# Low halves of weights by accumulating DMA, seven Strassen chunks in layer 0, and a new split of the modulation columns

## The chip, the cores and the metric

One Trainium2 chip; the program runs on one core. The metric is the device time of that core in microseconds (us), from runs of the whole program. TensorE is PE in the profile, VectorE DVE, ScalarE ACT, GpSimd POOL; SP is the queue from which almost all DMAs are issued.

## The reference

Two layers of an encoder trunk on 512 tokens of width 1024, all in float32. Each layer is a mixer (attention in two branches) and an MLP; both norms are modulated by `mod`, 6 x 1024 values for each layer that depend on `c` and `ada_w` alone.

```python
for l in range(DEPTH):
    mod = (cond @ ada_w[l] + ada_b[l])[:, None, :]
    shift_m, scale_m, gate_m, shift_f, scale_f, gate_f = jnp.split(mod, 6, axis=-1)
    h = rms_norm(x, norm_mix_g[l]) * (1.0 + scale_m) + shift_m
    proj = h @ w_in[l]
    ...
    x = x + gate_m * y
    h = rms_norm(x, norm_mlp_g[l]) * (1.0 + scale_f) + shift_f
    x = x + gate_f * (jnp.square(jax.nn.relu(h @ w_mlp_up[l])) @ w_mlp_down[l])
```

`w_mlp_up` is 1024 x 4096 and `w_mlp_down` 4096 x 1024.

## The kernel before

**Split operands.** PE multiplies in a format shorter than float32 (`R32`, fp32r). So each operand is held in two parts: a high part, rounded by a copy on ACT (`wh <- raw`), and the rest, subtracted on DVE (`wl <- raw, wh`). `split_w` does this for a weight block of 128 x 1024 (512 KB): SP loads `raw`, ACT writes `wh`, DVE writes `wl`. `mm3` makes a product from three matmuls: high by high, high by low, low by high. The pool of `raw` tiles has 4 buffers (`rawp`), that of `wh`, `wl` pairs 5 (`wp`).

**Columns.** `ada(l, j)` makes column j of the 48 columns of `mod`: SP loads 512 KB of `ada_w` into a `raw` tile, and DVE multiplies it by `cbc` and sums (`CUSTOM_DVE_ANT_0`, then a short read of the accumulator). Columns 0 to 15 of layer 1 must be there at the end of layer 0's MLP, the others at the end of layer 1's attention.

**Attention.** Each layer goes through some 60 slots in an order that is written out by hand for every engine (`order(True)`): parts of a projection, parts of attention of earlier slots, and what `mods` and `mods1` put at the slot's end. `mods1` gives layer 1 its columns 24 to 47, one at every second slot from 6 to 52.

**MLP.** 32 up tiles (`up_part`: 8 x 3 = 24 matmuls of 512 columns for each) are worked in 8 chunks of 4. What follows in a chunk is of one of two kinds, by `PLAIN[l] <= fc < 7`, with `PLAIN = (3, 0)`:

- A plain chunk: ReLU, square and split of the 4 tiles, then 8 sums over the 4 tiles in 96 matmuls; each result is multiplied by the gate on DVE and added to x on POOL. In layer 0 each of the chunks 0 to 2 ends with 8 columns of layer 1 (`INFF // PLAIN[l]`, 24 in all). The last chunk is plain in both layers.
- A Strassen chunk: `columnside` loads the four down blocks r11, r12, r21, r22 (r21 and r22 into the pool of `raw` tiles) and makes three differences of them on DVE. `rowside` makes and splits the row side. `down7` makes seven products of 12 matmuls each in the order r11, r21, t2, t1, t3, r22 and r21 - t2, splits the right side of each (`wsplit`: ACT, then DVE), and takes the results from PSUM on DVE into the sums `y` (`take`). Before `down7`, two up tiles of the next chunk are made.

Layer 0 had 4 such chunks (3 to 6), layer 1 had 7 (0 to 6). In the MLP no order is written out: a scheduler sets it when the program is built. Each engine then works its instructions in that fixed order, and waits on semaphores for the others; SP waits in the same way for a free buffer before it issues a load.

**PSUM.** `acc()` counts its calls and takes turns over 2 banks of one pool and 3 of another; `ubank()` gives up tiles others.

Of the kernel before, what the change touches and what calls it, by code (L numbers as in the profile page):

```python
# [10 lines left out]
F32 = mybir.dt.float32  # L11
R32 = mybir.dt.float32r
BF = mybir.dt.bfloat16
I32 = mybir.dt.int32
AF = mybir.ActivationFunctionType
OP = mybir.AluOpType
AX = mybir.AxisListType

DEPTH = 2
# [22 lines left out]
def trunk(ctx, tc, x, c, pos, cols, rows, ada_w, w_qkv, w_gate, w_ba, w_bb, w_out, w_up, w_down, out):  # L42
# [8 lines left out]
    rawp = pool("raw", 4)  # L51
    wp = pool("w", 5)
# [196 lines left out]
    def split_w(src, n=1024, scale=None, eng=None, spare=False):  # L249
        raw = rawp.tile([128, 1024], F32, name="raw", tag="raw")  # L250
        E_.dma_start(raw[:, :n], src)
        if spare:
            hi, lo = (big([128, 1024], R32, n_) for n_ in ("wh", "wl"))
        else:
            hi, lo = (wp.tile([128, 1024], R32, name=n_, tag=n_) for n_ in ("wh", "wl"))
        if scale is None:
            S_.activation(hi[:, :n], raw[:, :n], AF.Copy)
            (eng or V_).tensor_sub(lo[:, :n], raw[:, :n], hi[:, :n].bitcast(F32))
        else:
            S_.activation(hi[:, :n], raw[:, :n], AF.Copy, scale=scale)  # L260
            V_.scalar_tensor_tensor(lo[:, :n], raw[:, :n], scale, hi[:, :n].bitcast(F32),
                                           op0=OP.mult, op1=OP.subtract)
        return hi, lo

    def mm3(o, sh, sl, mh, ml, start, stop, **more):
# [331 lines left out]
    TURN = 18  # L597
    FIRST = 0
    AHEAD = 4
    PLAIN = (3, 0)  # L600
    INFF = 24

    def halves(hT):

# [111 lines left out]
    for l in range(DEPTH):  # L716
# [97 lines left out]
            loads.setdefault((k - 1, 1), []).append(slots[k]["load"])  # L814
        mods = {k: 16 + i for i, k in enumerate(range(54, 62))}
        MODS = len(mods)
        mods1 = {6 + 2 * i: INFF + i for i in range(48 - INFF)}
        post1_at, post2_at, turn_at = {}, {}, {}
        for k in range(nq):
            at = k + 1 if k >= done else STRIDE * k + done + FIRST  # L820
# [131 lines left out]

        def up_part(j, lo, hi):
            if j not in up:
                up[j] = [split_w(w_up[l, j])]
            if lo == 0:
                up[j].append(acc() if j < max(EARLY, FCH * PLAIN[l]) else ubank())
            (wh, wl), ps = up[j]
            hs = slice(lo, hi)
            for kt in range(KT):  # L960
                kc = slice(128 * kt, 128 * kt + 128)
                mm3(ps[:, hs], wh[:, kc], wl[:, kc], hF[kt][0][:, hs], hF[kt][1][:, hs], kt == 0, kt == KT - 1)
            return ps
# [15 lines left out]
        def product(banks, u, w, start):  # L979

            wh, wl = w
            for i, ps in enumerate(banks):
                for k in range(2):
                    tk = slice(256 * k + 128 * i, 256 * k + 128 * i + 128)
                    cw = slice(512 * k, 512 * k + 512)
                    mm3(ps, u[:, 0, tk], u[:, 1, tk], wh[:, cw], wl[:, cw], start and k == 0, k == 1,
                        skip_group_check=not start)
# [61 lines left out]
            V_.tensor_sub(r12, r22, r12)  # L1049
            return r11, r21, t2, t1, r12, r22  # L1050

        def down7(fc, u, b):

            def wsplit(raw):
                hi, lo = (wp.tile([128, 1024], R32, name=n_, tag=n_) for n_ in ("wh", "wl"))
                S_.activation(hi, raw, AF.Copy)
                V_.tensor_sub(lo, raw, hi.bitcast(F32))
                return hi, lo  # L1060

            r11, r21, t2, t1, t3, r22 = b

            def take(y, ps):
                if y not in ys:
                    ys[y] = [halfp.tile([128, 512], F32, name="y7", tag="half") for _ in range(2)]
                    for yt, b in zip(ys[y], ps):
                        S_.activation(yt, b, AF.Copy)
                else:
                    for yt, b in zip(ys[y], ps):  # L1070
                        V_.tensor_add(yt, yt, b)

            bank = lambda pool_, tag: [pool_.tile([128, 512], F32, name="acc", tag=tag) for _ in range(2)]
            xb, yb = bank(ssp, "s"), bank(tpp, "tp")
            if not zb:
                zb.extend(bank(accp, "acc"))
            product(xb, u[1], wsplit(r11), True)
            take((0, 0), xb)
            w21 = wsplit(r21)
            V_.tensor_sub(r21, r21, t2)  # L1080
            product(zb, u[2], w21, fc == PLAIN[l])
            product(xb, u[6], wsplit(t2), False)
            take((0, 1), xb)
            product(yb, u[5], wsplit(t1), True)
            take((1, 1), yb)
            product(xb, u[7], wsplit(t3), False)
            take((1, 1), xb)
            product(yb, u[3], wsplit(r22), False)
            take((0, 1), yb)
            product(xb, u[4], wsplit(r21), False)  # L1090
            take((1, 0), xb)

        for fc in range(FC):
            last = fc == FC - 1
            if seven(fc):
                w7 = columnside(fc)
            ups(fc, (2, 3) if fc and seven(fc - 1) else range(FCH))
            if fc == 0:
                gf = grow(l, 1)
            if seven(fc):  # L1100
                u7 = rowside(fc)
                ups(fc + 1, (0, 1))
                down7(fc, u7, w7)
                continue
            if last:
                for b, y in zip(zb, ys[0, 0]):
                    V_.tensor_add(y, y, b)
                for (i, cc), y2 in sorted(ys.items()):
                    for k, y in enumerate(y2):
                        xs = slice(512 * cc, 512 * cc + 512)  # L1110
                        V_.tensor_mul(y, y, gf[:, xs])
                        G_.tensor_add(x1[2 * i + k][:, xs], x1[2 * i + k][:, xs], y)
            if last and l + 1 < DEPTH:
                nxt = prepare(l + 1)
                for i in range(2):
                    nxt[1][0]["load"](i, True)
            for cc in range(2):
                w = [split_w(w_down[l, fc, cc, i]) for i in range(2)]
                if last and l + 1 < DEPTH and cc == 0:
                    nxt[1][0]["load"](2)  # L1120
                ahead = last and cc == 1 and l + 1 < DEPTH
                if ahead:
                    pairs = halves(nxt[0])
                    aT = affine(l + 1, 0)
                    norms = []
                    order(True)
                    nxt[1][0]["load"](3)
                for t in range(NT):
                    tk = slice(128 * t, 128 * t + 128)
                    d = sp.tile([128, 512], F32, name="d", tag="f512", bufs=6)  # L1130
                    final = last and l == DEPTH - 1 and cc == 1 and t == NT - 1
                    for lo, hi in ((0, 256), (256, 512)) if final else ((0, 512),):
                        ps = acc()[:, lo:hi]
                        for f in range(FCH):
                            wh, wl = w[f // 2]
                            cw = slice(512 * (f % 2) + lo, 512 * (f % 2) + hi)
                            mm3(ps, uT[f][:, 0, tk], uT[f][:, 1, tk], wh[:, cw], wl[:, cw], f == 0, f == FCH - 1)
                        xs = slice(512 * cc + lo, 512 * cc + hi)
                        V_.tensor_mul(d[:, lo:hi], ps, gf[:, xs])
                        (V_ if last else G_).tensor_add(x1[t][:, xs], x1[t][:, xs], d[:, lo:hi])  # L1140
                        if last and l == DEPTH - 1:
                            E_.dma_start(out[t, :, xs], x1[t][:, xs])
                    if last and l + 1 < DEPTH and cc == 0:
                        ms[t] = msp.tile([128, 2], F32, name="ms2", tag="ms")
                        square(x1[t], ms[t], 0)
                    if ahead:
                        norms.append(norm(l + 1, 0, t, x1[t], ms[t], aT, pairs))
                        if t > 1:
                            norms[t - 2][2]([0])
                        norms[t][0]()  # L1150
                        E_.dma_start(x2d[t], x1[t])
                        if t > 0:
                            norms[t - 1][1]()
                        if t > 1:
                            norms[t - 2][2]([1])
                if ahead:
                    norms[3][1]()
                    early = {1 + i: norms[2 + i][2] for i in range(2)}
            if l + 1 < DEPTH and not last:
                n = INFF // PLAIN[l]  # L1160
                for i in range(n * fc, n * fc + n):
                    ada(l + 1, i)


_ORDER = ["x", "c", "pos", "cols", "rows", "ada_w", "w_qkv", "w_gate", "w_ba", "w_bb", "w_out", "w_up",
# [64 lines left out]
```

## Time and profile before

| | |
|---|---|
| three runs | 1893.67, 1893.89, 1896.83 us; median 1893.89 |
| the profiled execution | 1896.49 us, of which the span of its instructions 1894.7 |
| busy, share of the span | PE 1857.2 us (98%), DVE 1382.4 (73%), ACT 934.6 (49%), POOL 407.0 (21%) |
| mean granted TensorE clock | 0.995 |
| HBM read | 205.09 MB |
| chain that ended last | PE 70%, DVE 15%, ACT 7%, DMA 3% |

By time: the first norm and projection up to about 95 us, layer 0's attention to 425, its gates and output projection to 600, its MLP to about 950, layer 1's attention to 1370, its gates and output projection to 1560, its MLP to the end.

PE's matmuls overlap in the profile (one of 512 columns shows as 389 ns, and one follows the other every 0.22 to 0.23 us), so a stretch of PE is judged by the number of matmuls in it. A group's mean is the mean time of one instruction; the idle time before it is the engine's wait, with what ended it.

### The profile page before, as it was taken

How to read it: one execution, taken by the hardware profiler on the slowest of the kernel's cores; microseconds unless marked ns; L12 is line 12 of the kernel's file. 1: busy time of each engine (PE TensorE's matmuls, PEld its weight loads, DVE VectorE, ACT ScalarE, POOL GpSimd, SP SyncE). 2: the span in 40 equal slices, each digit the busy share in tenths (PEclk: the TensorE clock that was granted, in tenths of full speed). 3: DMA queues.
4: the chain of work that ended last, by engine and by line, in shares of the span. 5: the costliest groups of instructions: out<-in, count | busy, mean ns of one | idle time of the engine just before them, and what ended most of it. 6: DMA issues, size and time to landing. Idle time of an engine off the chain costs nothing.

```text
span 1894.7 us, 27435 instructions
## 1 busy us (share of the span) xinstructions
PE 1857.2 (98%) x10012; PEld 1636.7 (86%) x10012; DVE 1382.4 (73%) x2721; ACT 934.6 (49%) x2009; POOL 407.0 (21%) x463
## 2 busy tenths in 40 slices
PE   7999999999999999999998999999999999999999
PEld 5999999998878888888898999988888888888887
DVE  8776678886586767688977676888743457788887
ACT  5555566666334432544454545666662345444441
POOL 4332324332121223000243231332310100000002
PEclk9999999999999999999999989999999999999999
DMA  7321111225583656322233231232232333332322
GB/s 297 138 68 58 52 54 48 70 65 156 181 288 122 200 189 205 96 89 89 78 123 121 86 112 57 84 101 81 66 112 89 100 126 107 104 108 89 111 68 88
DMA packets 63640, 212.10 MB, mean 112 GB/s; under 512 B 7185, under 2 KB 7569, under 8 KB 63506
## 3 DMA queue, kind: packets, MB, share of 16 engines
q1 hardware_dynamic: 63218, 210.27, 34.6%
q8 instruction: 79, 1.29, 0.3%
q14 instruction: 55, 0.45, 0.1%
q10 hardware_dynamic: 288, 0.09, 0.0%
HBM read 205.09 MB, written 5.24 MB: 111 GB/s over the span
## 4 chain that ended last, share of the span: by engine, by line
PE 70%; DVE 15%; ACT 7%; DMA 3%; issue 2%; POOL 2%; SPq 0%; ACTq 0%; DVEq 0%; POOLq 0%
PE acc L81 61%; PE tp L81 3%; DVE wl L81 3%; PE s L81 3%; DVE raw L81 2%; ACT p L81 2%; ACT wh L81 2%; PE pvb L81 2%; PE pv L81 2%; DVE T L81 1%; DVE kl L81 1%; DVE y L81 1%; DVE ms L81 1%; DVE nm L81 1%; POOL rs L81 1%
## 5 line engine op out<-in xcount | busy, mean ns | idle before, releaser
L81 PE MATMUL acc<-wh,hT 128*128 128x384 f32 x1792 | 518.5, 347 | 9.0 <-ACT hT L81 5.2
L81 DVE TENSOR_TENSOR wl<-raw,wh 128x1024 fp32r<-128x1024 f32 (+1 forms) x325 | 381.6, 1182 | 182.9 <-ACT wh L81 179.7
L81 PE MATMUL acc<-hT,wh 128*128 128x512 f32 (+1 forms) x1632 | 481.6, 378 | 0.0
L81 ACT ACTIVATE wh<-raw 128x1024 fp32r<-128x1024 f32 (+1 forms) x325 | 315.7, 986 | 331.3 <-PE acc L81 217.7
L81 PEld LDWEIGHTS acc<-hT,wh 128*128 128x128 f32 x1632 | 298.5, 188 | 54.6
L81 PEld LDWEIGHTS acc<-wh,hT 128*128 128x128 f32 x1792 | 330.6, 189 | 16.0 <-ACT hT L81 6.6
L81 PE MATMUL acc<-hT,wl 128*128 128x512 f32 (+1 forms) x816 | 306.0, 378 | 1.3 <-DVE wl L81 1.3
L81 PE MATMUL acc<-wl,hT 128*128 128x384 f32 x896 | 303.6, 339 | 3.7 <-DVE wl L81 3.7
L81 PE MATMUL acc<-wh,uT 128*128 128x512 f32 (+1 forms) x944 | 296.1, 388 | 0.2 <-DVE d L81 0.2
L81 POOL TENSOR_TENSOR rs<-ms,half_neg 128x4 f32<-128x4 f32 (+1 forms) x128 | 123.1, 962 | 493.5 <-DVE ms L81 492.3
L81 PEld LDWEIGHTS acc<-wh,uT 128*128 128x128 f32 x944 | 176.8, 188 | 37.3 <-DVE d L81 0.6
L81 PE MATMUL acc<-wl,uT 128*128 128x512 f32 (+1 forms) x472 | 182.5, 387 | 0.0
L81 PEld LDWEIGHTS acc<-hT,wl 128*128 128x128 f32 x816 | 153.5, 188 | 30.8 <-DVE wl L81 2.6
L81 PEld LDWEIGHTS acc<-wl,hT 128*128 128x128 f32 x896 | 169.7, 189 | 9.2 <-DVE wl L81 6.6
L81 DVE CUSTOM_DVE_ANT_0 raw<-raw,cbc,colt 128x1024 f32<-128x1024 f32 x94 | 123.5, 1322 | 18.2 <-DMA raw<-in_ada_w 17.9
L81 ACT ACTIVATE p<-s,nm 128x512 f32<-128x512 f32 x128 | 86.9, 684 | 86.7 <-DVE nm L81 86.7
L81 POOL TENSOR_TENSOR xt<-xt,y 128x512 f32<-128x512 f32 x16 | 26.2, 1651 | 461.3 <-DVE y L81 461.3
L81 PEld LDWEIGHTS acc<-wl,uT 128*128 128x128 f32 x472 | 88.6, 188 | 17.9
L81 DVE TENSOR_REDUCE nm<-s 128x1 f32<-128x512 f32 x128 | 82.1, 682 | 16.4 <-PE s L81 16.3
L81 ACT ACTIVATE sq<-acc 128x256 f32<-128x256 f32 x112 | 43.2, 385 | 87.2 <-DVE kl L81 67.7
L81 PE MATMUL s<-k,q 128*128 128x512 f32 (+1 forms) x224 | 84.8, 386 | 1.3 <-DVE n L81 1.3
L81 ACT ACTIVATE wT<-tp 128x512 f32<-128x512 f32 (+1 forms) x128 | 65.8, 541 | 39.7 <-PE tp L81 39.5
(157 smaller groups left out, 2884.3 us busy)
## 6 DMA issues: line engine op xcount, KB each, us to landing
raw<-in_ada_w SPq DMA_DIRECT2D x96, 512.0 KB, 4.1
raw<-in_w_qkv SPq DMA_DIRECT2D x112, 384.0 KB, 3.1
raw<-in_w_up SPq DMA_DIRECT2D x64, 512.0 KB, 3.8
raw<-in_w_down SPq DMA_DIRECT2D x64, 512.0 KB, 3.5
raw<-in_w_gate SPq DMA_DIRECT2D x32, 512.0 KB, 3.6
raw<-in_w_ba SPq DMA_DIRECT2D x16, 512.0 KB, 3.6
raw<-in_w_out SPq DMA_DIRECT2D x16, 512.0 KB, 3.6
xt<-in_x SPq DMA_DIRECT2D x8, 512.0 KB, 6.2
```

What stands on the lines that cost most here:

```text
L81: ins = f(*a, **k)
```

## The change

Five things change.

1. `split_add` takes the place of `split_w` for the up tiles that `up_part` loads (29 of 32 in each layer; the first three are loaded elsewhere, as before). ACT writes `wh`, then a second ACT instruction writes -`wh` into `wl`, and a DMA issued by POOL adds the weight block from HBM onto `wl`. DVE has no part in it.
2. In `down7` the blocks r11 and r22, which are multiplied as they are loaded, are split in the same way.
3. `PLAIN = (0, 0)`: layer 0's chunks 0 to 2 become Strassen chunks, so that it has 7.
4. `INFF = 35`: layer 0's MLP makes 35 of layer 1's columns, five in each Strassen chunk, one after each of the first five takes as the code is written (`idle`).
5. Layer 1's attention makes the other 13, one at every fourth slot from 6 to 54.

```diff
+    def split_add(src):
+
+        raw = rawp.tile([128, 1024], F32, name="raw", tag="raw")
+        E_.dma_start(raw, src)
+        hi, lo = (wp.tile([128, 1024], R32, name=n_, tag=n_) for n_ in ("wh", "wl"))
+        S_.activation(hi, raw, AF.Copy)
+        S_.activation(lo, hi.bitcast(F32), AF.Copy, scale=-1.0)
+        G_.dma_start(lo, src, accum_op=OP.add)
+        return hi, lo
...
-    PLAIN = (3, 0)
-    INFF = 24
+    PLAIN = (0, 0)
+    INFF = 35
...
-        mods1 = {6 + 2 * i: INFF + i for i in range(48 - INFF)}
+        mods1 = {6 + 4 * i: INFF + i for i in range(48 - INFF)}
...
-                up[j] = [split_w(w_up[l, j])]
+                up[j] = [split_add(w_up[l, j])]
...
-        def down7(fc, u, b):
+        def down7(fc, u, b, rest):
...
-            def wsplit(raw):
+            def wsplit(raw, src=None):
                 hi, lo = (wp.tile([128, 1024], R32, name=n_, tag=n_) for n_ in ("wh", "wl"))
                 S_.activation(hi, raw, AF.Copy)
-                V_.tensor_sub(lo, raw, hi.bitcast(F32))
+                if src is None:
+                    V_.tensor_sub(lo, raw, hi.bitcast(F32))
+                else:
+                    S_.activation(lo, hi.bitcast(F32), AF.Copy, scale=-1.0)
+                    G_.dma_start(lo, src, accum_op=OP.add)
                 return hi, lo
+
+            def idle():
+                if rest:
+                    rest.pop(0)()
...
-            product(xb, u[1], wsplit(r11), True)
+            product(xb, u[1], wsplit(r11, w_down[l, fc, 0, 0]), True)
             take((0, 0), xb)
+            idle()
...
-            product(yb, u[3], wsplit(r22), False)
+            product(yb, u[3], wsplit(r22, w_down[l, fc, 1, 1]), False)
             take((0, 1), yb)
+            idle()
...
-                down7(fc, u7, w7)
+                down7(fc, u7, w7, [lambda i=i: ada(l + 1, i) for i in range(5 * fc, 5 * fc + 5)] if l + 1 < DEPTH else [])
...
-            if l + 1 < DEPTH and not last:
-                n = INFF // PLAIN[l]
-                for i in range(n * fc, n * fc + n):
-                    ada(l + 1, i)
```

In the built program this makes 86 DMAs on POOL (58 up tiles and 28 down blocks) and 86 more instructions on ACT for the negations; PE has 36 matmuls less. The scheduler then puts the MLP in an order of its own. Three places of that order, with the numbers of the tiles; `wh_N` and `wl_N+1` are the halves of one block.

ACT before, in chunk 4 of layer 0, from the split of t3 (raw_8333) over r22 (raw_8337) and r21 - t2 (raw_8336) to the next up tiles and r11 (raw_8641):

```order
L81 ACTIVATE wh_8587<-raw_8333 128x1024
L81 ACTIVATE r_8509<-acc_8484 128x512
L81 ACTIVATE wh_8605<-raw_8337 128x1024
L81 ACTIVATE wh_8623<-raw_8336 128x1024
L81 ACTIVATE wh_8656<-raw_8654 128x1024
L81 ACTIVATE wh_8691<-raw_8689 128x1024
L81 ACTIVATE wh_8754<-raw_8752 128x1024
L81 ACTIVATE wh_8789<-raw_8787 128x1024
L81 ACTIVATE wh_8825<-raw_8641 128x1024
```

ACT now, at that place of chunk 2 of layer 0 (a plain chunk before), from the split of r22 (raw_7703) over r21 - t2 (raw_7702) to three of the four up tiles:

```order
L81 ACTIVATE wh_7988<-raw_7703 128x1024
L81 ACTIVATE r_7879<-acc_7854 128x512
L81 ACTIVATE wl_7989<-wh_7988 128x1024
L81 ACTIVATE wh_8010<-raw_7702 128x1024
L81 ACTIVATE wh_8043<-raw_8041 128x1024
L81 ACTIVATE wl_8044<-wh_8043 128x1024
L81 ACTIVATE wh_8079<-raw_8077 128x1024
L81 ACTIVATE wl_8080<-wh_8079 128x1024
L81 ACTIVATE wh_8143<-raw_8141 128x1024
L81 ACTIVATE wl_8144<-wh_8143 128x1024
```

Behind each split of an up tile, and of r22, stands its negation; the next split waits for both.

DVE before, in chunk 4 of layer 0 again, from the split of r21 - t2 (wl_8624) on: takes, and between them the splits of the next chunk's up tiles (wl_8657, wl_8692, wl_8755, wl_8790):

```order
L81 TENSOR_TENSOR wl_8624<-raw_8336,wh_8623 128x1024
L81 TENSOR_TENSOR y7_8272<-y7_8272,acc_8514 128x512
L81 TENSOR_TENSOR y7_8252<-y7_8252,acc_8512 128x512
L81 TENSOR_TENSOR y7_8253<-y7_8253,acc_8513 128x512
L81 TENSOR_TENSOR y7_8273<-y7_8273,acc_8515 128x512
L81 TENSOR_TENSOR wl_8657<-raw_8654,wh_8656 128x1024
L81 TENSOR_TENSOR y7_8252<-y7_8252,acc_8514 128x512
L81 TENSOR_TENSOR wl_8692<-raw_8689,wh_8691 128x1024
```

DVE now, between chunks 1 and 2 of layer 0, from the end of the takes: three columns (ISA, two instructions for each), the split of r21 (wl_7909), the square of an up tile, a low half of the row side, the difference r21 - t2, and the next two columns:

```order
L81 TENSOR_TENSOR y7_7365<-y7_7365,acc_7553 128x512
L81 ISA raw_7943,modT1_105<-raw_7943,cbc_96,colt_101 128x1024
L81 ISA modT1_105 128x1
L81 ISA raw_7964,modT1_105<-raw_7964,cbc_96,colt_101 128x1024
L81 ISA modT1_105 128x1
L81 TENSOR_TENSOR wl_7909<-raw_7702,wh_7908 128x1024
L81 SCALAR_TENSOR_TENSOR q7_7745<-acc_7718,r_7743 128x512
L81 TENSOR_TENSOR uT_7786<-q7_7515,uT_7786 128x512
L81 TENSOR_TENSOR raw_7702<-raw_7702,raw_7701 128x1024
L81 ISA raw_7985,modT1_105<-raw_7985,cbc_96,colt_101 128x1024
L81 ISA modT1_105 128x1
L81 ISA raw_8007,modT1_105<-raw_8007,cbc_96,colt_101 128x1024
```

Where splits of up tiles stood there are now columns; the first of the five stands just ahead of these rows. The code has the columns between the products, the built order has them together, behind the takes.

PE before, in chunk 4 of layer 0, inside the product of r22 (wh_8605): two matmuls of the next chunk's first up tile (wh_8656), then the product of t3 (wh_8587):

```order
L81 MATMUL acc_8514<-wl_8606,uT_8437 128x512
L81 MATMUL acc_8514<-wh_8605,uT_8437 128x512
L81 MATMUL acc_8660<-hT_6432,wh_8656 128x512
L81 MATMUL acc_8660<-hT_6433,wh_8656 128x512
L81 MATMUL acc_8512<-wh_8587,uT_8433 128x512
L81 MATMUL acc_8512<-wl_8588,uT_8433 128x512
```

The tile's third matmul, the first to read its low half wl_8657, followed after 18 others. PE now, in chunk 2, behind the product of t1 (wl_7947): two matmuls of the next chunk's first up tile, and the product of t3 (wh_7967):

```order
L81 MATMUL acc_7885<-wl_7947,uT_7797 128x512
L81 MATMUL acc_7885<-wh_7946,uT_7797 128x512
L81 MATMUL acc_8048<-hT_6432,wh_8043 128x512
L81 MATMUL acc_8048<-hT_6433,wh_8043 128x512
L81 MATMUL acc_7882<-wh_7967,uT_7801 128x512
L81 MATMUL acc_7882<-wl_7968,uT_7801 128x512
```

The two read `wh_8043` alone. The up tile's other 22 matmuls, the first of which reads `wl_8044`, now follow after 38 others: the products of t3, r22 and r21 - t2 (12 each) and two matmuls of the second up tile.

More of the change, by code (lines that the diff above doesn't have):

```diff
@@ L1083, in down7 @@
             take((0, 1), xb)
+            idle()
             product(yb, u[5], wsplit(t1), True)
             take((1, 1), yb)
+            idle()
             product(xb, u[7], wsplit(t3), False)
             take((1, 1), xb)
-            product(yb, u[3], wsplit(r22), False)
+            idle()
+            product(yb, u[3], wsplit(r22, w_down[l, fc, 1, 1]), False)
             take((0, 1), yb)
+            idle()
             product(xb, u[4], wsplit(r21), False)
```

## The prediction

> **What bounds the kernel now.** I read the slices of the page first, then busy time by stretches, one Strassen chunk or one group of attention slots to a stretch. Columns: the stretch and its length, busy us (xinstructions) of PE, PEld, DVE, ACT and POOL, granted clock, DMA share, GB/s.
>
> ```profile
> 663.00:757.00 94.00, 94.00 (x416) 77.88 (x415) 67.89 (x86) 27.50 (x35) 27.62 (x17) 1.00 0.62 197
> 1655.40:1695.80 40.40, 40.40 (x180) 33.42 (x179) 34.39 (x43) 17.25 (x22) 0.00 (x0) 1.00 0.35 105
> 1695.80:1736.20 40.40, 40.40 (x180) 33.45 (x179) 33.95 (x43) 17.25 (x22) 0.00 (x0) 1.00 0.34 103
> 281.60:309.70 28.10, 28.10 (x186) 26.96 (x185) 22.75 (x62) 19.43 (x58) 10.75 (x14) 1.00 0.19 57
> 309.70:338.00 28.30, 28.30 (x186) 27.16 (x185) 22.83 (x62) 19.49 (x59) 10.74 (x14) 1.00 0.19 57
> 1211.70:1242.00 30.30, 29.37 (x186) 27.07 (x185) 25.16 (x67) 19.48 (x59) 10.96 (x16) 1.00 0.29 88
> 1242.00:1272.00 30.00, 29.08 (x186) 26.82 (x185) 24.86 (x65) 19.20 (x58) 10.78 (x14) 1.00 0.30 89
> 989.60:1032.30 42.70, 38.16 (x231) 35.78 (x230) 32.00 (x88) 18.00 (x49) 16.57 (x20) 1.00 0.39 125
> 1053.00:1085.00 32.00, 32.00 (x235) 31.52 (x234) 19.89 (x61) 16.88 (x41) 7.64 (x10) 1.00 0.22 66
> 1089.50:1136.90 47.40, 45.75 (x267) 44.33 (x267) 33.97 (x100) 21.66 (x55) 16.03 (x20) 0.89 0.37 111
> 521.10:568.50 47.40, 44.90 (x194) 36.22 (x193) 42.10 (x56) 17.96 (x22) 12.37 (x6) 0.96 0.84 288
> ```
>
> Row 1 is a little over two plain chunks of layer 0, rows 2 and 3 are single Strassen chunks of layer 1. PE has no gap in either: 180 matmuls in 40.40 us are 0.224 us each, and the plain stretch runs at 0.226. In the MLP only PE's own count sets the time; DVE, at 34 of 40.4 us, is the next engine. Rows 4 to 7 are the same four attention slots with the same 186 matmuls: layer 0, which loads no columns there, needs 28.2 us, and layer 1, with two columns in each group, 30.15. There DVE does reach PE.
>
> **The change part by part.** Durations of one instruction (count | busy, mean ns | idle before):
>
> ```profile
> L81 DVE TENSOR_TENSOR wl<-raw,wh 128x1024 fp32r<-128x1024 f32 x54 | 65.6, 1222 | 26.7 <-ACT wh L81 25.4 <-DMA raw<-in_w_down 1.0
> L81 DVE SCALAR_TENSOR_TENSOR q<-acc,r 128x512 f32<-128x512 f32 x20 | 13.6, 682 | 0.0
> L81 DVE CUSTOM_DVE_ANT_0 raw<-raw,cbc,colt 128x1024 f32<-128x1024 f32 x16 | 20.5, 1282 | 11.6 <-DMA raw<-in_ada_w 11.4
> L81 DVE DVE_READ_ACCUMULATOR2_ANT modT<- 128x1 f32 x94 | 7.5, 80 | 0.0
> L81 ACT ACTIVATE wh<-raw 128x1024 fp32r<-128x1024 f32 x213 | 224.6, 1060 | 327.7 <-PE acc L81 216.7 <-DMA raw<-in_w_up 64.2 <-DMA raw<-in_w_down 11.5
> L81 POOL TENSOR_TENSOR rs<-ms,half_neg 128x4 f32<-128x4 f32 x112 | 113.0, 1009 | 492.3 <-DVE ms L81 492.3
> L81 POOL TENSOR_TENSOR xt<-xt,d 128x512 f32<-128x512 f32 x24 | 40.0, 1697 | 97.9 <-DVE d L81 97.9
> ```
>
> *Three more Strassen chunks in layer 0.* The down part of a plain chunk is 2 x 4 x 4 x 3 = 96 matmuls of 512 columns, of a Strassen chunk 7 x 12 = 84. 3 x 12 = 36 fewer, all on a PE without a gap: 36 x 0.224 = **-8.1 us**. Layer 1 enters its MLP the same way already, so I take no entry cost.
>
> *Eleven columns out of layer 1's attention.* Two columns cost 30.15 - 28.2 = 1.95 us in a group of four slots, 0.97 each. Slots 8, 12, ... 52 lose theirs (twelve), slot 54 gains one. The six of slots 32 to 52 lie in such groups: 5.8, less 0.97 for slot 54, is 4.9. The other six are bounded by 0 (the stretch 1053 to 1085 has columns and no gap in PE) and 5.8; PE does idle in the stretch 989.6 to 1032.3, where two of them lie, so I take 1.3. Together **-6.2 us**, bounds -4.9 to -10.7. Layer 1's slots also get other PSUM banks, since layer 0 calls acc() 33 times less; the rotation over five banks stays, so 0, bounds 1.5 us either way, a third of PE's 4.5 idle us in the stretch 989.6 to 1032.3.
>
> *DVE and ACT.* A Strassen chunk gives up four up splits and two direct ones, 6 x 1.22 = 7.3 us; a chunk of layer 0 takes five columns, 5 x 1.36 = 6.8. So 26.7 of 40.4 us in layer 1 and 33.5 in layer 0: no more than PE hides now, in sum. ACT goes from 17.3 to 17.3 + 6 x 1.06 = 23.6. In the MLP all this is worth 0, since nothing waited for DVE; without the relief three more chunks with columns would ask DVE for 40.8 of 40.4 us.
>
> *The chain of an add.* wl now comes from the split on ACT, its negation on ACT (1.06), POOL's issue, and a DMA that reads 512 KB again. No accumulating DMA and no DMA of POOL is in the trace. Nearest rows (us from issue to landing; the two lower rows are of 620 to 760 us and of 520 to 570 us, the latter a stretch at 0.84 DMA share):
>
> ```profile
> raw<-in_w_up SPq DMA_DIRECT2D x64, 512.0 KB, 3.8
> raw<-in_w_down SPq DMA_DIRECT2D x64, 512.0 KB, 3.5
> xt<-in_x SPq DMA_DIRECT2D x8, 512.0 KB, 6.2
> raw<-in_ada_w SPq DMA_DIRECT2D x24, 512.0 KB, 4.1
> raw<-in_ada_w SPq DMA_DIRECT2D x11, 512.0 KB, 5.0
> ```
>
> Below: 3.5, a plain load, with nothing for POOL. Above: 6.2 and the longest POOL row, 1.7: 7.9. I take 6.0, the 5.0 of the busy stretch and a small POOL instruction of 1.0. What it may take is counted in PE's order: an up tile's first two matmuls read wh alone, then follow 12 + 12 + 2 + 12 = 38 others before wl is read, 8.5 us, less the negation, leaves 7.5. So it lands in time with 1.5 us over: **0 us**; at 7.9 it is 0.4 late per chunk, 6 us over 14 chunks. On POOL nothing but other adds stands behind it. Behind a negation on ACT stand the next splits, which PE reads later than the add.
>
> *The columns' loads in layer 0.* DVE stands in line: a column whose load is late holds up every later split and take. On SP the columns are issued between the up tiles and the next chunk's four w_down blocks, two of which go out only when the fourth and the fifth column are done; DVE wants these last of all in the chunk, so I charge them nothing. Two of the four raw buffers are held by w_down blocks, so a chain of three loads with their landing L goes through each chunk: the r21 split frees a buffer, an up tile is loaded and split (ACT, 1.06), a column is loaded into it, then the column two later, whose end frees the buffer of the fifth. Between them on DVE stand four columns (5.4), 3.8 us of other work, and after the fifth seven instructions of 1024 (8.5) and fifteen of 512 (10.2) up to the next such split. The means count overlap twice: a chunk of layer 1 is 15 x 1.22 + 27 x 0.68 = 36.7 by them and 34.1 in rows 2 and 3, a factor 0.93. So 0.93 x 27.9 + 1.06 + 3 L = 27.0 + 3 L against 40.4: it holds up PE if L is over 4.5. L was 4.1 at 0.62 DMA share and 5.0 at 0.84. A chunk now moves 13 loads and 6 adds, 19 x 0.524 MB in 40.4 us = 246 GB/s, between the rows of 197 and 288. I take L = 4.65: 0.5 us a chunk, six chunks, **+3 us**; bounds 0 (L = 4.1) and 9 (L = 5.0).
>
> [...] No run here shows an add yet.
>
> *Sum*, against the profiled execution, 1896.49 us (span 1894.7 and 1.8 around it): -8.1 - 6.2 + 3 = -11.3. That execution is 2.6 above the median 1893.89, and it has one slice at clock 0.89; I assume as many such slices after. From the median: **1882.5 us**; 1876 to 1889 with the terms at their bounds, though not all at once.
>
> **The rivals.**
> - *Columns hold up DVE more* (L = 5.2 to 6.0). For: 3.8 us spent on this chain at every chunk, and DVE already waited 11.4 us for columns in row 1's plain chunks. Against: layer 0's plain chunks moved 197 GB/s with PE full. Price 6 x (2.1 to 4.5) = 13 to 27 in place of 3: 1892 to 1906, most likely 1895.
> - *Adds land late, slower.* Place: the third matmul of each up tile, and the second of the r22 block, in all 14 chunks. It costs from 7.5 us after issue, and eats the gain (11.3 / 14 = 0.8) from 8.3. For: nothing here shows an add; POOL's issue and a second operand come on top of a load. Against: no plain landing of this size is over 6.2. At 9.5 us: 14 x 2.0 = 28, so 1910; each further us 14 more.
> - *More than forecast*: L stays at 4.1 and the early columns give more: 1872 to 1876.
> - *The MLP part does nothing by itself*: DVE is not waited for there. That is in the forecast already; only PE's 36 matmuls and the moved columns pay.
>
> [...]
>
> **How the numbers follow.** Chances: forecast (1876 to 1889) 0.52, columns 0.24, late adds 0.20, more than forecast 0.04. The range 1876 to 1903 holds the forecast, most of the columns' case (0.22) and a little of the late adds (0.06). About 0.2%, 3.8 us, is what a measurement of this kernel can tell from no change: faster is below 1890.1, slower above 1897.7. The columns' case splits 0.06 faster, 0.09 same, 0.09 slower; the late adds 0.01 same and 0.19 slower. So faster 0.62, same 0.10, slower 0.28.
>
> **What would show it.** PE's matmul count 36 lower. A Strassen chunk of layer 1 still 40.4 us with 180 matmuls: if longer, with PE waiting for a DMA of wl, adds are late. A chunk of layer 0 at 40.4 to 41; if 42 to 45, and DVE idle before columns for their DMA while PE waits for y takes, the columns are. Landing of the adds under 7.5 us, of the columns under 5. Groups of layer 1's slots 32 to 52 near 29.2 us. Wrong altogether if the attention groups do not shorten, or if ACT, not DVE, is what PE waits for.

## The result and the profile after

The changed kernel takes **1938.63 us** (median of 4 runs, 1933.60 to 1940.65) against 1893.99 us for the kernel before on the same chip: a ratio of 1.022, 95% interval 1.020 to 1.025. It is slower; the forecast was 1882.5 us, with a range up to 1903.

Single Strassen chunks of layer 1 (rows 1 and 2) and two groups of four attention slots of layer 1 (rows 3 and 4), by the view of busy time in stretches, with the columns of the prediction:

```profile
1694.00:1738.70 44.70, 42.83 (x183) 34.94 (x182) 27.55 (x36) 23.36 (x30) 5.21 (x6) 0.96 0.68 165
1738.70:1781.00 42.30, 41.18 (x182) 33.74 (x181) 27.54 (x36) 23.20 (x30) 5.22 (x6) 1.00 0.66 160
1239.40:1268.40 29.00, 28.65 (x186) 27.00 (x185) 23.84 (x64) 19.31 (x59) 10.73 (x15) 1.00 0.24 73
1268.40:1297.40 29.00, 28.65 (x186) 26.99 (x185) 23.85 (x64) 19.32 (x59) 10.75 (x15) 1.00 0.24 74
```

The attention groups came down from 30.15 to 29.0 us. The chunks of layer 1 went the other way, from 40.40 us to 42.3 and 44.7, though DVE is less busy in them (27.5 us, was 34): PE now has gaps, and in the first row its clock is below 1. Layer 0's MLP is worse. The same stretch of it before and after:

```profile
640.00:930.00 290.00, 289.78 (x1278) 239.68 (x1277) 226.21 (x281) 110.20 (x142) 50.82 (x31) 1.00 0.43 136
```

```profile
640.00:930.00 290.00, 265.45 (x1116) 212.92 (x1114) 201.95 (x281) 146.43 (x182) 32.66 (x37) 0.97 0.80 213
```

In the same 290 us PE does 1116 matmuls in place of 1278, and the DMA share is 0.80 in place of 0.43. PE's groups in each MLP, with the idle time ahead of them and what ended it (the first four rows are layer 0, 640 to 960 us, the last two layer 1, 1610 to 1860 us):

```profile
L81 PE MATMUL acc<-hT,wh 128*128 128x512 f32 x429 | 137.0, 401 | 11.0 <-DVE q L81 10.9
L81 PE MATMUL acc<-wh,uT 128*128 128x512 f32 x392 | 128.4, 398 | 11.9 <-DVE y L81 7.9 <-DVE uT L81 3.9
L81 PE MATMUL acc<-hT,wl 128*128 128x512 f32 x214 | 84.3, 399 | 1.3 <-DMA wl<-in_w_up 1.3
L81 PE MATMUL acc<-wl,uT 128*128 128x512 f32 x196 | 77.5, 396 | 3.1 <-DMA wl<-in_w_down 3.1
...
L81 PE MATMUL acc<-hT,wl 128*128 128x512 f32 x171 | 68.3, 404 | 10.6 <-DMA wl<-in_w_up 10.6
L81 PE MATMUL acc<-wl,uT 128*128 128x512 f32 x168 | 65.3, 390 | 0.6 <-DMA wl<-in_w_down 0.6
```

The two layers lose time in two ways. In layer 1 PE waits for the add onto an up tile. In layer 0 it waits mostly for DVE (squares `q`, takes `y`, `uT`), and DVE in its turn for the columns' loads (row 1, 640 to 960 us). The rows of DMA issues for the whole run follow it:

```profile
L81 DVE CUSTOM_DVE_ANT_0 raw<-raw,cbc,colt 128x1024 f32<-128x1024 f32 x33 | 41.9, 1282 | 64.5 <-DMA raw<-in_ada_w 51.1 <-issue 6.9 <-ACT wh L81 3.8
...
raw<-in_ada_w SPq DMA_DIRECT2D x96, 512.0 KB, 5.3
...
wl<-in_w_up POOLq DMA_DIRECT2D x58, 512.0 KB, 8.4
...
wl<-in_w_down POOLq DMA_DIRECT2D x28, 512.0 KB, 7.1
```

An add lands 7.1 to 8.4 us after its issue, where I took 6.0. The page's queues (packets, MB, share of 16 engines) show the adds' price:

```profile
q1 hardware_dynamic: 63218, 210.27, 33.0%
q0 software_dynamic: 12384, 45.09, 12.9%
```

q0 holds the adds alone. One add takes 0.129 x 1938.9 us / 86 = 2.9 us of all sixteen engines; q1's transfers, nearly all of them loads, take 0.330 x 1938.9 us / 210.27 MB = 3.04 us for each MB, 1.6 for the same 0.524 MB. In the trace's records of single packets, the median of 4096 bytes takes 0.328 us in q0 and 0.159 in q1. So an add costs 1.8 times a load of its size by the shares and 2.06 times by the packets; what in the transfer makes it dearer, no run here shows.

How early each add was issued is found by setting the program's order beside PE's starts: the time from POOL's issue to the matmul that first reads `wl`. In the chunk of layer 1 from 1714.8 us on these are:

| add | issued at us | `wh` first read after us | `wl` first read after us | PE waited us |
|---|---|---|---|---|
| r22 | 1714.8 | 6.5 | 6.7 | 0 |
| first up tile | 1724.1 | -0.1 | 6.9 | 1.87 |
| second up tile | 1725.0 | 0.8 | 12.7 | 0 |
| third up tile | 1727.1 | 15.7 | 16.1 | 0 |
| fourth up tile | 1731.3 | 18.7 | 19.2 | 0 |
| r11 | 1735.0 | 13.2 | 13.5 | 0 |

The r22 add is issued with no other in flight, and lands 5.4 to 5.8 us after its issue in the seven chunks of layer 1. The up tiles' adds follow one another closely: in the six chunks of layer 1 that make four of them, the first lands after 5.8 to 8.4 us and the third after 10.7 to 11.7.

One of six is late, the first up tile. The timeline there (start, duration, engine; a row of two matmuls is x2):

```profile
1721.66 1.06 ACT L81 ACTIVATE wh<-raw 128x1024 fp32r<-128x1024 f32 x1 [0.94 <-DMA raw<-in_w_up]
1722.63 1.99 ACT L81 ACTIVATE wl<-wh 128x1024 fp32r<-128x1024 f32 x2
1724.07 1.82 POOL L81 DMA_DIRECT2D wl<-in_w_up  x2 [8.40 <-PE acc L81]
...
1731.01 0.50 PE L81 MATMUL acc<-hT,wl 128*128 128x512 f32 x1 [1.87 <-DMA wl<-in_w_up]
1731.34 0.62 PE L81 MATMUL acc<-hT,wh 128*128 128x512 f32 x2
1731.80 0.40 PE L81 MATMUL acc<-hT,wl 128*128 128x512 f32 x1
1732.04 1.02 PE L81 MATMUL acc<-hT,wh 128*128 128x512 f32 x2
1732.86 0.63 PE L81 MATMUL acc<-hT,wl 128*128 128x512 f32 x1
```

PE runs out of work 5.1 us after the issue (at 1729.14), the add lands 6.9 us after it, and then there is a second charge: from 1732.04 on the matmuls start at half the pace, one every 0.41 to 0.43 us where it was 0.23. The granted clock of the trace stands at 0.5 for 3.413 us there, three times in layer 1's MLP and for five such intervals in layer 0's; the kernel before has none in its MLPs. By the timeline layer 1's MLP has 13.0 us of PE gaps over 0.8 us, and three half-clock intervals lose 5.1 more: 18.1, for 17.6 by which its MLP is longer than without adds (below). Layer 0: the gaps of the four rows, 27.3, and 8.5 are 35.8, for 34.4.

### The profile page after: what moved, and what is told of

Read it like the earlier page. It is cut to its first block, busy times and chain, and to the rows that moved or that the text cites. A ratio compares the mean times of both kernels' runs of the same rounds, so it can differ in the third digit from the quotient of the medians.

```text
span 1938.9 us, 27647 instructions
## 1 busy us (share of the span) xinstructions
PE 1863.8 (96%) x9976; PEld 1634.8 (84%) x9976; DVE 1320.8 (68%) x2689; ACT 1032.9 (53%) x2113; POOL 440.4 (23%) x525
## 3 DMA queue, kind: packets, MB, share of 16 engines
q1 hardware_dynamic: 63218, 210.27, 33.0%
q0 software_dynamic: 12384, 45.09, 12.9%
## 4 chain that ended last, share of the span: by engine, by line
PE 54%; DVE 20%; DMA 12%; ACT 8%; issue 4%; POOL 1%; ACTq 0%; DVEq 0%; POOLq 0%; SPq 0%
PE acc L81 45%; DMA raw<-in_ada_w 5%; DVE wl L81 5%; DVE raw L81 3%; PE tp L81 3%; ACT wh L81 3%; DMA wl<-in_w_up 3%; PE s L81 3%; ACT p L81 2%; PE pv L81 2%; PE pvb L81 2%; DVE y L81 2%; DMA raw<-in_w_up 1%; DVE T L81 1%; DVE kl L81 1%
## 5 line engine op out<-in xcount | busy, mean ns | idle before, releaser
L81 PE MATMUL acc<-hT,wh 128*128 128x512 f32 (+1 forms) x1632 | 489.4, 384 | 11.0 <-DVE q L81 10.9
L81 ACT ACTIVATE wh<-raw 128x1024 fp32r<-128x1024 f32 (+1 forms) x334 | 325.1, 986 | 263.2 <-PE acc L81 200.9
L81 DVE TENSOR_TENSOR wl<-raw,wh 128x1024 fp32r<-128x1024 f32 (+1 forms) x248 | 279.2, 1132 | 170.4 <-ACT wh L81 160.6
L81 PEld LDWEIGHTS acc<-hT,wh 128*128 128x128 f32 x1632 | 302.5, 191 | 70.0 <-DVE q L81 14.0
L81 PE MATMUL acc<-hT,wl 128*128 128x512 f32 (+1 forms) x816 | 310.6, 384 | 14.8 <-DMA wl<-in_w_up 14.3
L81 PEld LDWEIGHTS acc<-hT,wl 128*128 128x128 f32 x816 | 155.9, 191 | 48.4 <-DMA wl<-in_w_up 17.7
L81 DVE TENSOR_TENSOR y<-y,acc 128x512 f32<-128x512 f32 x156 | 103.3, 682 | 59.1 <-PE acc L81 59.1
L81 POOL DMA_DIRECT2D wl<-in_w_down x28 | 24.6, 877 | 362.1 <-ACT wl L81 171.0
L81 POOL DMA_DIRECT2D wl<-in_w_up x58 | 51.1, 881 | 196.3 <-PE acc L81 95.6
L81 ACT ACTIVATE wl<-wh 128x1024 fp32r<-128x1024 f32 x86 | 90.4, 1058 | 1.9
```

The costliest lines, as they stand in the source:

```text
L81: ins = f(*a, **k)
```

## The experiments

Stages in us of each profiled run, cut at events of the timeline: an MLP goes from the transposes of its modulation to ACT's last read of an up tile, layer 1's attention from the end of layer 0's MLP to the transposes of its gates. Ratios are to the kernel before, timed beside each.

| kernel | median us | ratio, 95% interval | MLP 0 | attention 1 | MLP 1 |
|---|---|---|---|---|---|
| before | 1893.99 | | 298.9 | 576.8 | 290.2 |
| after | 1938.63 | 1.022, 1.020 to 1.025 | 328.1 | 567.4 | 307.7 |
| e1 adds only | 1927.66 | 1.019, 1.014 to 1.023 | 317.1 | 578.7 | 311.8 |
| e2 no adds | 1882.38 | 0.993, 0.992 to 0.995 | 293.7 | 565.1 | 290.1 |
| e3 copies for adds | 1896.75 | 1.000, 0.999 to 1.002 | 297.9 | 570.8 | 289.9 |
| e4 columns not loaded | 1918.96 | 1.013, 1.010 to 1.016 | 308.4 | 565.6 | 308.7 |
| e5 add on r11 | 1894.76 | 1.000, 0.999 to 1.001 | 304.5 | 569.9 | 290.1 |
| e6 r11, up tiles 3 and 4 | 1941.92 | 1.024, 1.020 to 1.027 | 332.4 | 571.6 | 307.7 |
| e7 r22, up tiles 1 and 2 | 1908.28 | 1.006, 1.005 to 1.008 | 317.4 | 570.0 | 288.8 |
| e8 as e5, columns not loaded | 1879.47 | 0.992, 0.990 to 0.994 | 290.4 | 566.3 | 290.2 |
| e9 as e2, columns not loaded | 1878.46 | 0.991, 0.989 to 0.993 | 290.1 | 565.1 | 290.2 |
| e10 adds in layer 1 alone | 1886.42 | 0.995, 0.993 to 0.996 | 293.6 | 565.7 | 288.8 |

In before, attention 1 holds a half-clock stretch of 10.24 us, 5.1 us lost. The runs of e1, e3, e5, e6 and e7 hold the same stretch there, those of after, e2, e4, e8, e9 and e10 none. Without it attention 1 takes 564.8 to 567.4 us in every run from after on but e1.

**e1: the adds alone, on the chunks and columns of before.**

```diff
-    PLAIN = (0, 0)
-    INFF = 35
+    PLAIN = (3, 0)
+    INFF = 24
...
```

The columns stand where they stood before, at every second slot and behind the chunks.

> The adds alone, on the kernel before: up tiles and the blocks r11 and r22 come by adds, but layer 0 keeps its three plain chunks and columns go where they went before. Theory 'adds late' (an add's packet takes the DMA engine 327 ns where a copy takes 159, adds of one ring stand behind one another and land 6 to 10 us after issue, PE stops at the first matmul that reads wl): layer 1's MLP keeps the whole of its loss, so from the gate's transposes to the last up tile 305 to 310 us (290 before, 307.7 with the change), layer 0 loses about 2.5 us in each of four Strassen chunks, total 1915 to 1930. Theory 'columns' (all loss comes from column loads that hold up DVE): layer 1's MLP returns to 290, total 1890 to 1896.

In this run layer 0's MLP is 18.2 us longer than in before and layer 1's 21.6, with the columns in their old places. So the adds cost by themselves. This profiled run was the longest of the kernel's (1943.6 us), so its stages lie above the median's.

**e2: everything but the adds.**

```diff
-                up[j] = [split_add(w_up[l, j])]
+                up[j] = [split_w(w_up[l, j])]
...
-            product(xb, u[1], wsplit(r11, w_down[l, fc, 0, 0]), True)
+            product(xb, u[1], wsplit(r11), True)
...
-            product(yb, u[3], wsplit(r22, w_down[l, fc, 1, 1]), False)
+            product(yb, u[3], wsplit(r22), False)
```

> The change without its adds: every low half is subtracted on DVE again, with seven Strassen chunks in layer 0 and 35 columns there. Theory 'adds late': layer 1's MLP returns to 290 us; layer 0 asks DVE for 34.1 + 6.8 = 40.9 us a chunk against PE's 40.4, so it loses 0.5 to 2 us a chunk, and the total is 1880 to 1893. Theory 'columns': DVE is now fuller than with the change and waits for the same loads, so layer 0's MLP stays at 325 us or more (328 with the change, 299 before), total 1905 to 1925.

1882.38 us, 0.1 from the forecast and faster than both kernels. That it is as near as 0.1 is luck: the same program took 1884.46 us in e11. Seven Strassen chunks with five columns each hardly make PE wait, though DVE has all its splits back (640 to 930 us again):

```profile
640.00:930.00 290.00, 288.71 (x1271) 237.73 (x1270) 277.69 (x364) 125.20 (x164) 12.08 (x8) 1.00 0.51 160
```

DVE is busy 277.7 of 290 us and PE 288.7. In this stretch the relief that the adds were to give is worth 1.3 us at most, PE's idle time.

**e3: the same program with copies.** The accumulate flag goes, in both places where the code issues an add:

```diff
-        G_.dma_start(lo, src, accum_op=OP.add)
+        G_.dma_start(lo, src)
```

> The change, with a plain copy by the same DMA of POOL in place of the add, in the same order of instructions on every engine; wl then holds the weight itself instead of the rest. It tells the add from the POOL queue. Theory 'the add is a transfer of twice the length': packets of 159 ns, landing 4 to 5.5 us after issue, PE has no wait for wl, layer 1's MLP 290 to 293 us, total 1890 to 1912 with layer 0 still held up by columns. Theory 'POOL's queue is slow whatever it carries': landing stays at 7 to 10 us and the total within 1930 to 1940.

Same order on every engine, same DMAs, same bytes, 42 us less. The copies' rows:

```profile
q0 software_dynamic: 12384, 45.09, 7.5%
...
wl<-in_w_up POOLq DMA_DIRECT2D x58, 512.0 KB, 6.1
...
wl<-in_w_down POOLq DMA_DIRECT2D x28, 512.0 KB, 4.7
```

The queue's share is 7.5% where it was 12.9%, and the landing is 4.7 to 6.1 us, about the 6.0 that I took. The accumulation itself is what costs. What e3 costs over e2, 14 us, is 4.2 in layer 0's MLP, some 3 at the end of the kernel and 5.7 in attention, of which 5.1 is the half-clock stretch that e3's profiled run holds and e2's does not. One of e3's ten runs took 4698 us; I know no cause, and the interval leaves it out.

**e4: the columns of layer 0's MLP without loads.** The built order moves too.

```diff
-        E_.dma_start(raw, ada_w[l, j])
+        if load:
+            E_.dma_start(raw, ada_w[l, j])
...
-            ins = V_.tensor_tensor_reduce(raw, raw, cbc, 1.0, bias, OP.mult, OP.add, m)
+            ins = V_.tensor_tensor_reduce(raw, raw if load else cbc, cbc, 1.0, bias, OP.mult, OP.add, m)
```

> The change, with the 35 columns of layer 0's MLP made without their loads: DVE multiplies the resident cbc instead of a column of ada_w, so the modulation of layer 1 is not the reference's; DVE's work is the same, 17.5 MB less are loaded, and no column waits for a DMA. Theory 'columns': layer 0's MLP falls from 328 us to 295 to 303, layer 1's stays at 307, total 1903 to 1915. Theory 'adds late' in both layers: layer 0 falls only a little, to 318 or more, total 1925 or more.

Neither theory alone: layer 0 comes down by 19.7 us, and 18.3 are left over e9, which has neither adds nor loads of columns. What is left has the form of layer 1's loss. PE's groups of layer 0, 640 to 950 us:

```profile
L81 PE MATMUL acc<-hT,wl 128*128 128x512 f32 x222 | 87.5, 399 | 13.0 <-DMA wl<-in_w_up 13.0
L81 PE MATMUL acc<-wl,uT 128*128 128x512 f32 x206 | 80.1, 390 | 0.9 <-DMA wl<-in_w_down 0.9
```

Against e9 layer 0 loses 308.4 - 290.1 = 18.3 and layer 1 308.7 - 290.2 = 18.5. So without the columns' loads late adds cost each layer 18 us, and 34.4 - 18.3 = 16 of layer 0's loss in after come only with these loads. It is a difference between two built orders: in after itself PE waits only 4.4 us for `wl` in layer 0 (1.3 and 3.1 above), and the rest for DVE.

**e5: of the adds only r11's**, one for each chunk (the edits of e2 but for the line of r11).

> The version without adds, with one add put back in each Strassen chunk: block r11, whose product stands behind three or four up tiles (13 us from its negation to its use as counted in layer 0 of the change). Theory 'lateness' (an add costs only where it lands after PE asks for it): r11 lands in time, layer 1's MLP 290 to 291.5, layer 0 a little shorter than without adds since DVE is freed of 1.2 us a chunk, total 1878 to 1884. Theory 'dose' (every add costs by its engine time, 56 us over 86 adds or 0.65 each): 14 adds give 9 us, total 1889 to 1893.

Layer 1 loses nothing (290.1), layer 0 10.8 us. No row of PE waits for a DMA of `wl` there, and DVE waits 18.3 us for columns where without adds it waited 0.0 (640 to 950 us, e2 and then e5):

```profile
L81 DVE CUSTOM_DVE_ANT_0 raw<-raw,cbc,colt 128x1024 f32<-128x1024 f32 x33 | 42.1, 1282 | 0.0
L81 DVE CUSTOM_DVE_ANT_0 raw<-raw,cbc,colt 128x1024 f32<-128x1024 f32 x34 | 43.4, 1280 | 18.4 <-DMA raw<-in_ada_w 18.3
```

**e6 and e7: three adds of a chunk each.** By PE's order in after I called the first set roomy and the second tight.

```diff
-                up[j] = [split_add(w_up[l, j])]
+                up[j] = [(split_add if j % FCH >= 2 else split_w)(w_up[l, j])]
```

That is e6, with the add on r11; e7 has `j % FCH < 2` and the add on r22.

> Three adds in each chunk: r11 and the third and fourth up tile, which PE reaches 12 us or more after their negation; the first two up tiles and r22 are subtracted on DVE. Theory 'lateness': no wait of PE for wl in layer 1, its MLP 290 to 293, layer 0 at 293 to 300, total 1880 to 1890. Theory 'dose': half the adds, half the loss, total 1905 to 1915.

> The other three of the six: r22 and the first and second up tile come by adds, r11 and the later up tiles are subtracted on DVE. The same number of adds and the same traffic as the run before. Theory 'lateness': PE waits for wl of the first up tile of each chunk, layer 1's MLP 300 to 308, total 1900 to 1925, and above the run with the roomy three by 15 us or more. Theory 'dose': the same as the run with the roomy three within 5 us.

In layer 1 the place decides, but my labels were the wrong way round: e6 loses 17.6 us, all that six adds lose, and e7 nothing. The built order had moved. In e6 the tiles with an add are those that PE takes at once (`wh` read 1.0 to 1.6 us after the issue); in e7 the tiles split by DVE come first, and `wh` of the adds' tiles is read 10.7 and 15 us after. PE's waits in e6 and then in e7 (1610 to 1860 us):

```profile
L81 PE MATMUL acc<-hT,wl 128*128 128x512 f32 x180 | 71.3, 401 | 10.6 <-DMA wl<-in_w_up 10.6
```

```profile
L81 PE MATMUL acc<-hT,wl 128*128 128x512 f32 x192 | 73.9, 389 | 0.0
```

The count of matmuls between the first read of `wh` and that of `wl` is 16 for the late tile of e6 and 2 for e7's: it tells nothing without the time of the split.

In layer 0 both lose over e2, 38.7 us in e6 and 23.7 in e7, with three adds of a chunk in place of six. PE waits there for `wl` 4.6 and 2.7 us only (640 to 970 us), and DVE waits 38.8 and 23.3 us for columns' loads. Neither was run without these loads, so what the adds cost by themselves there stays open.

**e8 and e9: is it the columns' loads in layer 0?** e8 is e5 and e9 is e2, both with the edit of e4.

> As the kernel with adds on r11 alone (1894.8 us, MLP of layer 0 304.5 us), but the 35 columns in layer 0's MLP multiply a resident tile and are not loaded; their values, and so layer 1's modulation, are not the reference's. Theory 'the add costs layer 0 through the columns' loads': with no loads to delay, the seven adds of layer 0 cost nothing there, so its MLP is within 2 us of that of the kernel with no adds and no column loads. Theory 'the add is late for PE itself' (the r11 block is split when PE is about to read it): the adds still cost 8 to 11 us in layer 0, so its MLP is 8 to 11 us longer than that of the other kernel. Layer 1's MLP 290 us by both.

> As the kernel with no adds (1882.4 us, MLP of layer 0 293.7 us), but the 35 columns in layer 0's MLP are not loaded; layer 1's modulation is not the reference's. It is the base for the kernel beside it, and tests the columns' term: if the 2.9 us by which the MLP of layer 0 came out above PE's own count are the columns' loads, it is 290.8 us here (7 x 84 x 2 matmuls at the pace of layer 1's MLP, 290.1) and the total near 1879.5; if they are DVE's own work for the columns, it stays at 293.7 and the total near 1882.4.

Settled as far as one build of each can: r11's adds cost layer 0 10.8 us beside the loads and 0.3 without them. And e9 gives the columns' term of my sum: without their loads PE's stretch is full, and layer 0 takes 3.6 us less than in e2.

```profile
640.00:930.00 290.00, 290.00 (x1280) 239.85 (x1278) 279.38 (x360) 127.73 (x168) 13.90 (x8) 1.00 0.32 101
```

**e10: adds where they are early**, in layer 1 alone, on the first two up tiles and r22; then **e11 and e12**, e2 and e10 beside each other.

```diff
+                up[j] = [(split_add if l and j % FCH < 2 else split_w)(w_up[l, j])]
...
+            product(yb, u[3], wsplit(r22, w_down[l, fc, 1, 1] if l else None), False)
```

> The kernel with no adds in layer 0, and adds in layer 1 alone, on the first two up tiles of a chunk and the r22 block, which cost nothing in layer 1 when they stood in both layers (288.8 us against 290.1 without). Theory 'lateness' (a load that lands before PE needs it costs nothing): layer 0's MLP 293.7, layer 1's 288.5 to 290.5, total 1880 to 1883. Theory 'every add costs' (about 1 us each in layer 0 by the runs with one and three): 21 adds cost 10 us or more, 1892 or above.

> The kernel without adds once more, beside the one with adds in layer 1 alone on the same chip: 1881 to 1885 us, ratio to before 0.991 to 0.995.

> Adds in layer 1 alone, on the first two up tiles and the r22 block. Its first run lost nothing in the profiled stages, but its median was 4 us above that of the kernel without adds, measured on another chip at another time. Theory 'lateness': same time as the kernel without adds beside it, within 2 us. Theory 'every add costs': 4 us or more above it.

The first median, 1886.42, lay between the two expectations. Side by side e11 took 1884.46 us (ratio 0.994, 0.993 to 0.996) and e12 1882.92 (0.994, 0.993 to 0.995): 21 early adds cost nothing, and bring nothing that these runs can tell. Attention of layer 1, the same program in both, took 565.1 us in e2 and 569.7 in e11; e11's run holds the half-clock stretch of 10.24 us there, e2's none, and that is 5.1 us that comes and goes between runs of one program.

More buffers for `wl`, so that the splits could go further ahead, were not tried.

## Why the prediction was wrong

- **PE's 36 matmuls, -8.1: right.** Layer 0's MLP in e9 is 8.8 us under that of before.
- **Columns out of attention, -6.2: right.** 576.8 less the 5.1 of its half-clock stretch is 571.7; e2 has 565.1, so -6.6, and after 567.4, -4.3.
- **DVE and ACT, 0: right.** e2 and e9 show it more strongly than I argued: at 277.7 of 290 us DVE makes PE idle 1.3 us at most, and in e9, at 279.4, PE has no gap. My 40.8 of 40.4 us for a chunk without the relief was too high; e2's row gives 0.958 x 40.4 = 38.7.
- **The chain of an add, 0: the step that failed.** Three parts of it were wrong. (1) Landing: 6.0 taken from plain loads. An add on its own meets it (r22 in layer 1, 5.4 to 5.8); but adds in flight together take 7.1 to 8.4 as medians, and 5.8 to 8.4 for the first up tile of layer 1's chunks, the one that counts. (2) The time allowed, 7.5, was counted in layer 0's built order and priced for 14 chunks. In layer 1 of that same build 20 other matmuls, not 38, stand between the two reads; with the tile's own two that is 22 x 0.224 = 4.9, and PE ran dry 5.1 us after the issue. Those rows were there to be read, and 6.0 against 4.9, or against 3.9 less the negation, would have cost 1 to 2 us a chunk even with my landing. (3) The wait is not the whole price: after three of the gaps in layer 1's MLP PE ran at half clock for 3.413 us, 1.7 us lost each time. Together 18 us in layer 1, and as much in layer 0 when the columns' loads are away (e4).
- **The columns' loads, +3: right in size without adds, not by its mechanism.** e2 against e9 is 3.6. But in e2 these loads land in 3.5 us and DVE waits 0.0 us for them, so it isn't the chain 27.0 + 3 L; PE's waits there are small and of several kinds (ACT's splits 0.7, `uT` 0.7, `y` 0.5), and which one the loads cause stays open. With the adds L is 5.9 in layer 0, past all that I allowed for the forecast (5.0), and the cost is 16 us. The formula gives 27.0 + 17.7 - 40.4 = 4.3 a chunk, 26 for six; e5, at a median L of 4.1, under its threshold, lost 10.8. A median tells too little: DVE waited ten times for the 34 columns there.
- **The sum without the adds, -11.3: right** (e2: -12.7 against before's 1895.04 us beside it, -11.6 against the 1893.99 above).
- **Rivals.** The late adds were the right mechanism, with a chance of 0.20, and their price was too low: 14 x (8.4 - 7.5) = 13 us by its formula, some 36 measured (18.3 and 17.6). The columns' rival was right too, with 1892 to 1906 for it alone. I priced them one by one; both come from the adds' longer transfer (0.328 us for a packet of 4096 bytes, 0.174 as a copy in e3), and so came together.

What stays open: how layer 0's loss in after divides between late adds and delayed columns, and the 3 us that after, e1, e3 and e4 lose from the last up tile on (25.0 to 25.6 us, where before and e2 take 22.0 and 22.3). As e3 loses them too, the accumulation is not their cause.

## What to carry to other kernels

In these runs an accumulating DMA took 1.8 times a copy's engine time (12.9% of the engines against 7.5% for the same 86 transfers, after and e3). Price it so until a trace of your own kernel says otherwise, both for itself and for every load that shares the engines with it (the columns' loads of layer 0's MLP landed after 5.9 us in after and 3.5 in e2, as medians), and set its landing against the time from the issue to the first read, in each layer's own order. DVE, 96% busy in e2 but hardly ever waited for (PE idle 1.3 of 290 us at most), had no need of relief; moving its work onto a chain that PE waited for could here only cost. And a wait of PE can cost more than its length: 1.87 us of waiting in after was followed by 3.413 us at half clock.

## What the runs showed of the hardware

- The median packet of 4096 bytes took 0.328 us in an accumulating DMA (after), 0.174 in a plain one of the same queue (e3), and 0.159 in one of SP's loads (after).
- POOL spent 0.88 us on issuing an accumulating DMA and 0.54 on the same copy (after, then e3):

```profile
L81 POOL DMA_DIRECT2D wl<-in_w_up x58 | 51.1, 881 | 196.3 <-PE acc L81 95.6 <-ACT wl L81 57.1 <-DVE y L81 16.0
```

```profile
L81 POOL DMA_DIRECT2D wl<-in_w_up x58 | 31.5, 543 | 193.4 <-PE acc L81 90.3 <-ACT wl L81 67.8 <-DVE y L81 19.1
```

- In layer 1's MLP of after, gaps of 1.79 and 1.87 us on PE were followed by 3.4 us at half clock, gaps of 1.12 and 2.12 us were not.
- In each of the fourteen traces the half-clock intervals start on a grid of 3.413 us. Of the grid intervals at full clock between 45 and 1870 us, taken over all traces, each of the 29 in which PE idled over 1.9 us (by the profile's modelled ends) was followed by half clock, and none of some 7360 with under 1.6 us; between the two, 12 of 35 were. In before and after alone it is 6 of 6, none of 1038, and 4 of 9. The gap of 2.12 us, from 1816.00 to 1818.12 us of after, lies across a line of its grid, with 1.4 us before it and 0.7 behind. These are counts in the traces of these kernels; what sets the grid, no run shows.
